# The first load of a row-normalising kernel cut into 16 and 112 partitions, and one row of the first tile moved between two forms of scaling

## The chip, the cores and the metric

The kernel runs on one core of one Trainium2 chip. The metric is the device time of one execution in microseconds (us). Times are read from repeated runs; the profile is one further execution, recorded by the hardware profiler, and its span is the time from its first to its last instruction.

## What is computed

The input has 32 x 512 rows of 1024 float32 numbers. Every row is divided by the sum of its absolute values:

```python
batch, seq, dim = 32, 512, 1024
...
sums = np.sum(np.abs(x), axis=-1, keepdims=True)
return (x / (sums + 1e-8)).astype(np.float32)
```

So 67.11 MB are read from memory, 67.11 MB are written back, and each number is used once for its sum and once for the division.

## The kernel before

The 16384 rows are taken as 128 per partition and cut into 11 tiles. Tiles 0 to 9 hold 12 rows for each of the 128 partitions (48 KB in each partition, 6.3 MB in all), and tile 10 holds the last 8. Tiles 0, 1 and 10 share one region of 32 rows per partition; within a tile the rows of one partition lie together in memory. Four tile buffers (`BUFS = 4`) are used in turn, so tile 4 can only be loaded when tile 0 has been stored.

The order is written out by hand. First the loads of tiles 0 to 3 are issued; then for each tile follow `compute(i)`, `store(i)` and, while tiles are left, `load(i + BUFS)`. All loads are issued from SyncE (SP, line 87), all stores from ScalarE's queue (ACT, line 97). A load or a store waits for the semaphores of what it needs, and what stands behind it in its queue waits too.

`max_dma_last_dim` sets the size of one piece of a transfer (a descriptor, seen in the trace as one packet): `WHOLE` is 49152 bytes, one partition's 12 rows; `HALF` is 24576. Tiles 0 and 1 are loaded with `WHOLE`, so the load of tile 0 is 128 packets of 48 KB, one for each partition. The store of tile 0 is cut in two: its first three rows (`FIRST = 3`) in packets of 4 KB, the other nine in packets of 36 KB.

`normalize` works on one tile. VectorE (DVE) sums the absolute values of all rows (L47), adds epsilon (L54) and takes the reciprocal (L56). The scaling of the rows is then divided in three, by `split`: some rows in one VectorE instruction that multiplies by a broadcast reciprocal (L58), some in single-row VectorE instructions (L65), and some in single-row ScalarE instructions (L68). An entry `split[i] = (kt, ks)` gives the number of single VectorE rows and of ScalarE rows; the rest go into the one large instruction. For tile 0 it is `(3, 4)`: five rows in one instruction, three single rows on VectorE, four on ScalarE. The first part of tile 0's store needs rows 0 to 2, which the large instruction writes.

Of the kernel before, what the change touches and what calls it, by code (L numbers as in the profile page):

```python
# [1 line left out]

# [4 lines left out]

FP32 = mybir.dt.float32
EPS = 1e-8


@with_exitstack
def kernel(
    ctx: ExitStack,
    tc: tile.TileContext,
    x: bass.AP,
    out: bass.AP,
):
    nc = tc.nc
    P = nc.NUM_PARTITIONS  # L20

    x_flat = x.flatten_outer_dims()
    out_flat = out.flatten_outer_dims()
    n, d = x_flat.shape

    R = 12
    BUFS = 4
    HEAD = 32
    per_partition = n // P
    assert n % P == 0 and (per_partition - HEAD) % R == 0  # L30
    rows = [R] * ((per_partition - HEAD) // R + 2) + [HEAD - 2 * R]

    def piece(flat, i):
        head = flat[: P * HEAD, :].rearrange("(p r) d -> p r d", p=P)
        if i < 2:
            return head[:, R * i : R * (i + 1), :]
        if i == len(rows) - 1:
            return head[:, 2 * R :, :]
        a = P * (HEAD + R * (i - 2))
        return flat[a : a + P * R, :].rearrange("(p r) d -> p r d", p=P)  # L40

    sbuf = ctx.enter_context(tc.tile_pool(name="sbuf", bufs=BUFS))
    stats = ctx.enter_context(tc.tile_pool(name="stats", bufs=len(rows)))

    def normalize(x_tile, k, kv, kt):
        s = stats.tile([P, R], FP32)
        nc.vector.tensor_reduce(  # L47
            out=s[:, :k],
            in_=x_tile[:, :k, :],
            axis=mybir.AxisListType.X,  # L50
            op=mybir.AluOpType.add,
            apply_absolute_value=True,
        )
        nc.vector.tensor_scalar_add(out=s[:, :k], in0=s[:, :k], scalar1=EPS)  # L54
        inv = stats.tile([P, R], FP32)
        nc.vector.reciprocal(out=inv[:, :k], in_=s[:, :k])  # L56
        if kv:
            nc.vector.tensor_mul(  # L58
                out=x_tile[:, :kv, :],
                in0=x_tile[:, :kv, :],  # L60
                in1=inv[:, :kv].unsqueeze(2).to_broadcast([P, kv, d]),
            )
        for r in range(kv, kv + kt):
            row = x_tile[:, r, :]
            nc.vector.tensor_scalar_mul(out=row, in0=row, scalar1=inv[:, r : r + 1])  # L65
        for r in range(kv + kt, k):
            row = x_tile[:, r, :]
            nc.scalar.activation(  # L68
                out=row,
                in_=row,  # L70
                func=mybir.ActivationFunctionType.Copy,
                scale=inv[:, r : r + 1],
            )

    last = len(rows) - 1
    split = {0: (3, 4), 1: (0, 3), 2: (0, 3), last - 1: (0, 2), last: (4, 4)}

    tiles = {}

    HALF, WHOLE = 24576, 49152
    FIRST = 3

    def load(i):
        x_tile = tiles[i] = sbuf.tile([P, R, d], FP32, name="x_tile")
        nc.sync.dma_start(out=x_tile[:, : rows[i], :], in_=piece(x_flat, i), max_dma_last_dim=WHOLE if i < 2 else HALF)  # L87

    def store(i):
        if i == 0:  # L90
            parts = [(0, FIRST, 4 * d), (FIRST, R, WHOLE)]
        elif i == last - 2:
            parts = [(0, R // 2, HALF), (R // 2, R, HALF)]
        else:
            parts = [(0, rows[i], WHOLE if i >= last - 1 else HALF)]
        for a, b, size in parts:
            nc.scalar.dma_start(
                out=piece(out_flat, i)[:, a:b, :],
                in_=tiles[i][:, a:b, :],
                max_dma_last_dim=size,  # L100
            )

    def compute(i):
        k = rows[i]
        kt, ks = split.get(i, (0, 0))
        normalize(tiles[i], k, k - kt - ks, kt)

    with tc.manual_schedule():
        for i in range(BUFS):
            load(i)  # L110
        for i in range(len(rows)):
            compute(i)
            store(i)
            if i + BUFS < len(rows):
                load(i + BUFS)


# [1 line left out]
_INS = ['x']  # L119
_OUTS = [((32, 512, 1024), 'float32')]  # L120


# [23 lines left out]
```

## Time and profile before

| what | value |
|---|---|
| time, median of 3 runs | 316.62 us (316.51 to 316.66) |
| span of the profiled execution | 315.2 us |
| difference of the two | 1.4 us outside the span |
| DMA, mean rate over the span | 426 GB/s, 134.22 MB |
| packets of the loads (queue q1) | 2736 |
| packets of the stores (queue q10) | 3024 |
| VectorE busy | 260.6 us, 83% |
| ScalarE busy | 18.5 us, 6% |

The profiled execution has no time of its own beside its span; what lies around the span is taken as the 1.4 us between it and the median. The page's second part cuts the span into 40 slices of 7.9 us; a digit is the busy share of an engine in tenths, and the last row is what the DMA engines moved. In tables of stretches, each row gives for one stretch its length, the busy time of each engine (with the number of instructions), the granted clock of TensorE (which has no work here), the DMA share (1.00 is all 16 DMA engines busy) and the rate. A packet is put down in the stretch in which it begins, so that a stretch shorter than a packet can show a share above 1 or a rate of 0.

### The profile page before, as it was taken

What the parts mean: (1) busy time and instruction counts of PE and PEld (TensorE: products, weight loads), DVE (VectorE), ACT (ScalarE), POOL (GpSimd) and SP (SyncE); (2) the same over time, 40 slices, a digit from 0 to 9 for tenths busy, and PEclk for the clock granted to TensorE, in tenths of its full rate; (3) what the DMA queues carried; (4) which work ended last, traced back from release to release, by engine and by line L of the source; (5) the groups of instructions that cost most, each with busy time, mean ns of one, the idle gap of its engine ahead of it and who ended that gap; (6) DMA issues with size and microseconds to landing.
All of it is one profiled execution on the core that took longest, in us unless ns stands there. A gap on an engine that the chain in (4) does not pass through costs nothing.

```text
span 315.2 us, 172 instructions
## 1 busy us (share of the span) xinstructions
DVE 260.6 (83%) x50; ACT 18.5 (6%) x17; POOL 0.2 (0%) x4
## 2 busy tenths in 40 slices
DVE  0079999999999999989996997999699969999000
ACT  0010503004000000000000000000000000203200
POOL 0000000000000000000000000000000000000000
DMA  8999999999999999999999999999999999999997
GB/s 318 480 399 412 437 407 464 411 436 413 415 446 437 415 446 437 415 449 434 415 449 437 412 449 437 412 449 437 415 446 437 415 437 434 432 428 496 399 408 324
DMA packets 5761, 134.22 MB, mean 426 GB/s; under 512 B 385, under 2 KB 385, under 8 KB 769
## 3 DMA queue, kind: packets, MB, share of 16 engines
q1 hardware_dynamic: 2736, 67.11, 49.8%
q10 hardware_dynamic: 3024, 67.11, 49.4%
q14 instruction: 1, 0.00, 0.0%
HBM read 67.11 MB, written 67.11 MB: 426 GB/s over the span
## 4 chain that ended last, share of the span: by engine, by line
DVE 40%; DMA 33%; another core or an unknown queue 18%; ACT 1%; issue 0%; SPq 0%
DVE s L47 23%; DMA x_tile<-in_x_dram 17%; DMA out_dram<-x_tile 16%; DVE x_tile L58 15%; ACT x_tile L68 1%; DVE x_tile L65 1%; DVE inv L56 0%; DVE s L54 0%; SPq L87 0%
## 5 line engine op out<-in xcount | busy, mean ns | idle before, releaser
L47 DVE TENSOR_REDUCE s<-x_tile 128x12 f32<-128x12288 f32 (+1 forms) x11 | 138.2, 12562 | 29.8 <-DMA x_tile<-in_x_dram 29.8
L58 DVE TENSOR_TENSOR x_tile<-x_tile,inv 128x12288 f32<-128x12288 f32 (+3 forms) x10 | 113.6, 11358 | 0.5
L68 ACT ACTIVATE x_tile<-x_tile,inv 128x1024 f32<-128x1024 f32 x16 | 17.2, 1138 | 256.9 <-DVE inv L56 256.9
L65 DVE TENSOR_SCALAR x_tile<-x_tile,inv 128x1024 f32<-128x1024 f32 x7 | 4.8, 749 | 0.0
L56 DVE RECIPROCAL inv<-s 128x12 f32<-128x12 f32 (+1 forms) x11 | 2.5, 226 | 0.4
L68 ACT ACT_TABLE_LOAD x1 | 1.3, 1283 | 17.8 <-DMA x_tile<-in_x_dram 17.8
L54 DVE TENSOR_SCALAR s<-s 128x12 f32<-128x12 f32 (+1 forms) x11 | 1.9, 174 | 0.4
L130 POOL MEMSET const-bfloat16-1.0<- 128x1 bf16 x1 | 0.1, 101 | 0.0
L130 POOL MEMSET const-uint8-127<- 128x1 uint8 x1 | 0.1, 101 | 0.0
L130 POOL MEMSET const-float32-0.0<- 128x1 f32 x1 | 0.1, 98 | 0.2 <-issue 0.2
L130 POOL MEMSET const-float32-1.0<- 128x1 f32 x1 | 0.1, 98 | 0.0
## 6 DMA issues: line engine op xcount, KB each, us to landing
x_tile<-in_x_dram SPq DMA_DIRECT2D x10, 6144.0 KB, 36.9
out_dram<-x_tile ACTq DMA_DIRECT2D x8, 6144.0 KB, 49.1
out_dram<-x_tile ACTq DMA_DIRECT2D x2, 3072.0 KB, 33.4
out_dram<-x_tile ACTq DMA_DIRECT2D x1, 4608.0 KB, 37.9
x_tile<-in_x_dram SPq DMA_DIRECT2D x1, 4096.0 KB, 32.2
out_dram<-x_tile ACTq DMA_DIRECT2D x1, 4096.0 KB, 20.9
out_dram<-x_tile ACTq DMA_DIRECT2D x1, 1536.0 KB, 29.3
```

Source lines behind the costliest of these rows:

```text
L47: nc.vector.tensor_reduce(out=s[:, :k], in_=x_tile[:, :k, :], axis=mybir.AxisListType.X, op=mybir.AluOpType.add, apply_absolute_value=True,)
L54: nc.vector.tensor_scalar_add(out=s[:, :k], in0=s[:, :k], scalar1=EPS)
L56: nc.vector.reciprocal(out=inv[:, :k], in_=s[:, :k])
L58: nc.vector.tensor_mul(out=x_tile[:, :kv, :], in0=x_tile[:, :kv, :], in1=inv[:, :kv].unsqueeze(2).to_broadcast([P, kv, d]),)
L65: nc.vector.tensor_scalar_mul(out=row, in0=row, scalar1=inv[:, r : r + 1])
L68: nc.scalar.activation(out=row, in_=row, func=mybir.ActivationFunctionType.Copy, scale=inv[:, r : r + 1],)
L130: nc = _bacc.Bacc("TRN2", target_bir_lowering=False, num_devices=1)
```

## The change

The load of tile 0 becomes two DMAs from the same queue: partitions 0 to 15 first, then partitions 16 to 127, still with 48 KB packets, one for each partition. The other loads and all stores are as they were. In the scaling of tile 0 the large VectorE instruction takes six rows instead of five, and two single rows instead of three are left on VectorE.

```diff
-    split = {0: (3, 4), 1: (0, 3), 2: (0, 3), last - 1: (0, 2), last: (4, 4)}
+    split = {0: (2, 4), 1: (0, 3), 2: (0, 3), last - 1: (0, 2), last: (4, 4)}
...
     FIRST = 3
+    AHEAD = 16
 
     def load(i):
         x_tile = tiles[i] = sbuf.tile([P, R, d], FP32, name="x_tile")
-        nc.sync.dma_start(out=x_tile[:, : rows[i], :], in_=piece(x_flat, i), max_dma_last_dim=WHOLE if i < 2 else HALF)
+        cuts = [(0, AHEAD), (AHEAD, P)] if i == 0 else [(0, P)]
+        for a, b in cuts:
+            nc.sync.dma_start(
+                out=x_tile[a:b, : rows[i], :],
+                in_=piece(x_flat, i)[a:b],
+                max_dma_last_dim=WHOLE if i < 2 else HALF,
+            )
```

## The prediction

> **What bounds the kernel now.** I read the page's busy times and slices first. VectorE works in 83% of the span, the DMA row stands at 9 in all but the first and the last slice.
>
> ```profile
> DVE 260.6 (83%) x50; ACT 18.5 (6%) x17; POOL 0.2 (0%) x4
> ...
> DMA  8999999999999999999999999999999999999997
> ```
>
> Then the busy time by stretches, to see whether the DMA engines ever wait for VectorE.
>
> ```profile
> 0.00:16.00 16.00, 0.00 (x0) 0.00 (x0) 0.20 (x4) 1.00 0.95 393
> ...
> 62.00:64.00 2.00, 2.00 (x1) 0.00 (x0) 0.00 (x0) 1.00 1.12 371
> 64.00:66.00 2.00, 2.00 (x1) 0.00 (x0) 0.00 (x0) 1.00 1.00 416
> 66.00:76.00 10.00, 9.90 (x4) 0.77 (x1) 0.00 (x0) 1.00 1.00 433
> ...
> 100.00:280.00 180.00, 167.18 (x26) 2.19 (x2) 0.00 (x0) 1.00 1.00 432
> ...
> 293.00:314.00 21.00, 0.00 (x0) 0.22 (x1) 0.00 (x0) 1.00 0.92 396
> ```
>
> The share is 1.00 for 180 us on end, at 432 to 433 GB/s. That is 27.1 GB/s for each of 16 engines, so a 48 KB packet takes 49152 B / 27.1 = 1.815 us, and 134.22 MB take 134.22 / 0.433 = 310.0 us. Of the 315.2 us span 5.2 are left: the start before the first packet, the landing of the last, and some slow packets. In the last 21 us VectorE does nothing and the DMA engines still drain stores: the last store is issued at 293.25 us by the timeline, 20 us before the end. So the time is that of the DMA engines. What VectorE does is covered by their queues; what delays the DMA engines in the first tile is never made up, because nothing later has slack.
>
> The chain of waits says the same for the start, and that the first tile has no compute beside it.
>
> ```profile
> 0.73 17.05 DMA x_tile<-in_x_dram
> 17.78 0.02 issue
> 17.80 12.96 DVE s L47
> ```
>
> Last I look at the first microseconds by themselves: the queues in 0 to 3 us, then short stretches.
>
> ```profile
> q1 hardware_dynamic: 16, 0.79, 84.9%
> ```
>
> ```profile
> 1.00:1.50 0.50, 0.00 (x0) 0.00 (x0) 0.00 (x0) 1.00 0.00 0
> 1.50:1.75 0.25, 0.00 (x0) 0.00 (x0) 0.00 (x0) 1.00 2.61 786
> 1.75:2.00 0.25, 0.00 (x0) 0.00 (x0) 0.00 (x0) 1.00 5.83 1769
> 2.00:2.50 0.50, 0.00 (x0) 0.00 (x0) 0.00 (x0) 1.00 0.88 295
> 2.50:3.00 0.50, 0.00 (x0) 0.00 (x0) 0.00 (x0) 1.00 0.00 0
> ```
>
> Packets are put down where they begin. Sixteen 48 KB packets, one per engine, begin between 1.5 and 2.5 us, about 1 us after the issue at 0.73; three of them (295 GB/s x 0.5 us = 0.147 MB) only after 2.0. The next packets begin after 4.0 us, so the first ones take over 2 us.
>
> **The change part by part.** *The scaling of tile 0.* The rows, by shape:
>
> ```profile
> L58 DVE TENSOR_TENSOR x_tile<-x_tile,inv 128x9216 f32<-128x9216 f32 x2 | 19.5, 9758 | 0.1
> ...
> L58 DVE TENSOR_TENSOR x_tile<-x_tile,inv 128x5120 f32<-128x5120 f32 x1 | 5.5, 5491 | 0.0
> L65 DVE TENSOR_SCALAR x_tile<-x_tile,inv 128x1024 f32<-128x1024 f32 x7 | 4.8, 749 | 0.0
> ```
>
> One row costs 9758/9 = 1.08 us to 5491/5 = 1.10 us in L58 and 0.75 in L65. Six rows take 6.5 to 6.6 us, 1.05 more; one single row less saves 0.75. Tile 0's scaling ends 0.3 us later and the first store, which waits for L58, is issued 1.05 us later (36.78 before). Behind it in ScalarE's queue stand the second part of that store, moved by 0.3, and the ScalarE rows of tile 1, which start at 52.1 us. At 36.8 us the loads of tiles 1 to 3 still fill the engines: four loads are 4 x 14.5 = 58 us of work, and with the store of tile 0 the engines are supplied to about 74 us, while tile 1 is stored at 62. I put this edit at 0. If the cover were gone it would cost 0.3 to 1.05 us. VectorE's 0.3 us goes into its own waits for loads: 29.8 us in six waits, 17.8 of them the first, so 12 later on.
>
> *The issue.* SP issues one DMA more. Its issues stand 0.42 us apart at the start (0.37 to 0.61 us each), so the loads of tiles 1 to 3 are issued some 0.4 us later, and the 112 partitions at about 1.1 us. Their packets would reach the engines by about 2.1 to 2.6 us, and the first ones are in work until 4.0: covered, 0. Each engine also ends one more DMA; packets of 4 bytes are all that adds.
>
> *The start of the first packets.* Sixteen descriptors instead of 128 may be handed out sooner. The first packets begin between 1.5 and 2.5 us, so the most that all could gain is some 0.6 us, and the least is nothing, or a loss of one issue, 0.4 us. I take a gain of 0.2.
>
> *The place of the first packets.* This is what I think decides. In every transfer of the trace 128 partitions take part, so the sixteen packets under way can lie all over SBUF, and the sum is 433 GB/s in every stage. The first piece puts sixteen packets on sixteen neighbouring partitions at the same moment. One partition takes a packet at the full 27.1 GB/s of an engine. Whether neighbours share a way in, no row shows. One end: they share nothing, the sixteen packets take 1.8 us, cost 0. The other: all sixteen share one way of 27.1 GB/s, 16 x 1.815 = 29.0 us, cost 27. The row that is nearest in size, the sixteen packets of the first 3 us, is spread over the partitions, which is the one thing that differs, so it can't choose. I take the middle in ratio, a factor of four: groups of four neighbours share, 4 x 1.815 = 7.3 us, **5.4 us more** on every engine, as each holds one of these packets at the head of its queue.
>
> [...]
>
> *The other 112.* With ways of 27.1 GB/s and 433 in all there are 16 ways, so 8 partitions to each. The first piece has used half of four of them; the other twelve still have 8 packets to take, 8 x 1.815 = 14.5 us where seven packets per engine alone are 12.7: 1.8 us more at the least, if the ways are never left idle. At the other end two engines always meet on one way, 12.7 us more. Engines that have drifted apart meet less, so I take 3.3, nearer to the lower end.
>
> Sum: 5.4 + 3.3 - 0.2 = 8.5 us. Against the profiled execution, 315.2 + 8.5 = 323.7 us of span, plus the 1.4 us outside it: 325.1, or 316.6 + 8.5 = **325.1 us**. Tile 0 would land at about 26 us instead of 17.8; VectorE, later by as much, has its 12 us of waits to give.
>
> **The rivals.** *Nothing shared (R1).* The packets of 48 KB go as fast to neighbours as elsewhere, or the rows keep the engines that they had in one transfer. For it speaks that a single partition takes the full rate, and that each engine has eight packets of tile 0 either way. Then only the start counts: 316.6 - 0.2 = 316.4, and it decides if the first sixteen packets end by 4.7 us as now. [...]
>
> *The start is worth more, and a stall goes (R2), on the faster side.* Between 62 and 66 us the rate is 371 and 416 instead of 433 GB/s: 62 and 17 GB/s too little for 2 us each, (124 + 34) / 433 = 0.36 us lost just when the loads run out and the first store ends. A first store that is 1.05 us later moves that meeting. With a start of 0.3 to 0.6 us earlier on the engine that is last now, 0.7 to 1.0 us in all: 315.8. Against it: the stall may as well grow by as much.
>
> *A small loss (R3).* The second load's packets come after the first have ended, or the 62 us stall doubles: 0.4 to 1 us, 317.4. It decides if engines idle between the two pieces, which the first packets' 2 us speak against.
>
> **How the numbers follow.** What a measurement of this kernel can tell is about 0.2%, 0.63 us. The place of the packets has most of the chance, 0.47, with its own range 320 to 329 (5.4 alone, less the start and some of the share, up to 5.4 + 7). R1 0.21, R2 0.27 and R3 0.05. R2 needs 0.63 us or more from a start and a stall that may each go either way; it stands above R1 because the rows hold up to 1 us to be won and R1's own 0.2 us would have to stay alone. So faster 0.28, same 0.20, slower 0.52. The range must hold both signs: 315.7 to 329.0 leaves out about 0.1 below (the better part of R2's upper gains) and 0.06 above.
>
> **What would show it.** If right, the first sixteen packets of the load queue end near 8 to 9 us instead of 4 to 4.7, so that the stretch from 4 to 8 us shows few new packets and a rate far below 400 GB/s; the chain's first DMA step is 24 to 29 us instead of 17.05; from 40 us on the rate is 432 again and the end is later by what was lost. L58 of tile 0 takes 6.5 us and nothing waits for it. If the first step of the chain stays at 17 us, sharing is refuted and R1 to R3 are left; then the first packets' starts and the rate in 62 to 66 us tell which. If tile 0 lands late and the end does not move, my view that nothing later has slack is wrong.

## The result, and the profile after

The changed kernel takes 331.86 us (median of 4 runs, 331.29 to 332.37) against 316.62: 15.24 us more, a ratio of 1.0482 (95% interval 1.047 to 1.0494). The profiled execution has a span of 330.1 us and a time of 331.71. Slower was forecast, by 8.5 us; the measured time lies above the range of 315.7 to 329.0 us that was given.

The page's busy times and slices, as before: busy share and number of instructions by engine, then 40 slices, now of 8.25 us each, with the DMA share in tenths and the rate.

```profile
DVE 261.0 (79%) x49; ACT 18.5 (6%) x17; POOL 0.2 (0%) x4
...
DMA  9997999999999999999999999999999999999896
GB/s 137 244 268 208 465 390 429 438 441 425 438 432 432 429 432 429 438 426 432 432 429 435 438 429 435 432 438 432 429 435 432 429 428 442 434 435 474 387 449 262
```

The rates of the kernel before, in its slices of 7.9 us:

```profile
GB/s 318 480 399 412 437 407 464 411 436 413 415 446 437 415 446 437 415 449 434 415 449 437 412 449 437 412 449 437 415 446 437 415 437 434 432 428 496 399 408 324
```

VectorE's work is what it was, 261.0 us. The DMA row alone would show next to nothing: the engines count as busy at 9, 9, 9 and 7 in the first four slices. The row under it shows the loss: 137 to 268 GB/s in these slices where the kernel before had 318 to 480, then the old 430 or so. With the share near 1 at half the rate, time in which a packet is held up counts as busy, so the busy share must be read with the rate.

The busy time by stretches of the changed kernel (length, busy time of DVE, ACT and POOL, clock, DMA share, GB/s):

```profile
0.00:16.00 16.00, 0.00 (x0) 0.00 (x0) 0.20 (x4) 1.00 1.02 194
16.00:32.00 16.00, 0.00 (x0) 0.00 (x0) 0.00 (x0) 1.00 0.94 243
32.00:36.00 4.00, 2.39 (x1) 1.28 (x1) 0.00 (x0) 1.00 0.92 393
...
62.00:64.00 2.00, 2.00 (x1) 0.00 (x0) 0.00 (x0) 1.00 1.01 434
64.00:66.00 2.00, 2.00 (x1) 0.00 (x0) 0.00 (x0) 1.00 1.04 444
...
100.00:280.00 180.00, 167.59 (x26) 0.00 (x0) 0.00 (x0) 1.00 1.00 432
```

The kernel before in the second of these stretches (the first, at 393 GB/s, stands in the prediction):

```profile
16.00:32.00 16.00, 14.10 (x4) 2.02 (x2) 0.00 (x0) 1.00 0.97 418
```

In the first 32 us 7.0 MB move where before 393 and 418 GB/s made 13.0 MB of them; the missing 6.0 MB are 13.8 us of work at 433 GB/s. From 40 us on the rate is back: 427 GB/s in 40 to 62 us (422 before) and 432 from 100 to 280 us, as before. The start of the chain of waits of the changed kernel (start, length, what):

```profile
1.17 32.34 DMA x_tile<-in_x_dram
...
33.61 12.96 DVE s L47
...
47.06 6.56 DVE x_tile L58
```

Tile 0 is summed from 33.6 us on instead of 17.8, 15.8 us later. The last packet of tile 0 ends 15.0 us later (at 32.5 us instead of 17.4), and the span is 14.9 us longer. The queue of the loads in the first 3 us of the changed kernel has the same sixteen packets and bytes as before:

```profile
q1 hardware_dynamic: 16, 0.79, 206.1%
```

The last number is the time of these packets as a share of 16 engines' 3 us: 2.061 x 3 = 6.2 us for each, where 84.9% meant 2.5. In the trace the last of them ends at 8.7 us instead of 4.75, and the 112 packets of the second piece follow with 3.29 us on average instead of 1.82. So for each engine the first packet costs 6.18 - 2.55 = 3.6 us more, and the seven others 23.0 - 12.7 = 10.3 us.

### The profile page after: what moved, and what is told of

Its sections match the earlier page's. It is cut to its first block, busy times and chain, and to the rows that moved or that the text cites. A ratio compares the mean times of both kernels' runs of the same rounds, so it can differ in the third digit from the quotient of the medians.

```text
span 330.1 us, 174 instructions
## 1 busy us (share of the span) xinstructions
DVE 261.0 (79%) x49; ACT 18.5 (6%) x17; POOL 0.2 (0%) x4
## 4 chain that ended last, share of the span: by engine, by line
DVE 38%; DMA 36%; another core or an unknown queue 17%; ACT 1%; SPq 0%; issue 0%; DVEq 0%
DVE s L47 22%; DMA x_tile<-in_x_dram 21%; DVE x_tile L58 15%; DMA out_dram<-x_tile 14%; ACT x_tile L68 1%; DVE inv L56 0%; DVE x_tile L65 0%; SPq L90 0%; DVE s L54 0%; DVEq L47 0%
## 5 line engine op out<-in xcount | busy, mean ns | idle before, releaser
L47 DVE TENSOR_REDUCE s<-x_tile 128x12 f32<-128x12288 f32 (+1 forms) x11 | 138.2, 12562 | 45.2 <-DMA x_tile<-in_x_dram 45.2
L58 DVE TENSOR_TENSOR x_tile<-x_tile,inv 128x12288 f32<-128x12288 f32 (+3 forms) x10 | 114.6, 11465 | 0.5
L68 ACT ACT_TABLE_LOAD x1 | 1.3, 1283 | 33.6 <-DMA x_tile<-in_x_dram 33.6
```

The source lines that it names most:

```text
L47: nc.vector.tensor_reduce(out=s[:, :k], in_=x_tile[:, :k, :], axis=mybir.AxisListType.X, op=mybir.AluOpType.add, apply_absolute_value=True,)
L58: nc.vector.tensor_mul(out=x_tile[:, :kv, :], in0=x_tile[:, :kv, :], in1=inv[:, :kv].unsqueeze(2).to_broadcast([P, kv, d]),)
L68: nc.scalar.activation(out=row, in_=row, func=mybir.ActivationFunctionType.Copy, scale=inv[:, r : r + 1],)
```

## The experiments

**Each edit alone.** The split alone, with one load of tile 0:

```diff
-    split = {0: (3, 4), 1: (0, 3), ...
+    split = {0: (2, 4), 1: (0, 3), ...
```

> Only the scaling of tile 0 is changed, to one instruction of six rows and two single rows; its load is one DMA as before. Theory A (the place: packets under way at the same moment to neighbouring partitions share a way into SBUF, and the scaling is hidden): 316.6 us, within 0.4 either way; tile 0 lands at 17.8 us. Theory B (the cut matters only together with the later first store): 318 us or more already here. The stall at 62 to 66 us (371 and 416 GB/s before) may move by up to 0.4 us in either direction.

Measured: 316.81 us (316.60 to 316.93), ratio 1.0005 (0.9997 to 1.0014). The split is no part of the 15 us. The stall of 62 to 66 us moved:

```profile
62.00:64.00 2.00, 2.00 (x2) 0.00 (x0) 0.00 (x0) 1.00 1.31 455
64.00:66.00 2.00, 2.00 (x1) 0.00 (x0) 0.00 (x0) 1.00 0.86 367
```

These are the two stretches with the split alone: 455 and 367 GB/s, in sum a loss of (66 x 2 - 22 x 2) / 433 = 0.2 us where before there were 0.36.

The cut alone, with the scaling as before (`split = {0: (3, 4), ...`, load as in the changed kernel):

> Only the load of tile 0 is cut, into partitions 0 to 15 and 16 to 127; the scaling is as before (five rows, three single ones). Theory A: 331.9 us within 0.6, the whole loss, tile 0 landing at 33 to 34 us. Theory B (both edits needed): clearly under 330.

Measured: 331.93 us, ratio 1.0483 (1.0469 to 1.0498), the whole loss.

**Cut by rows instead of partitions.**

```diff
-    AHEAD = 16
+    AHEAD = 2
...
-        cuts = [(0, AHEAD), (AHEAD, P)] if i == 0 else [(0, P)]
+        cuts = [(0, AHEAD), (AHEAD, R)] if i == 0 else [(0, rows[i])]
...
-                out=x_tile[a:b, : rows[i], :],
-                in_=piece(x_flat, i)[a:b],
+                out=x_tile[:, a:b, :],
+                in_=piece(x_flat, i)[:, a:b, :],
```

> The load of tile 0 is two DMAs again, but cut by rows: the first two rows of all 128 partitions (packets of 8 KB), then the other ten (packets of 40 KB). Scaling as before. Theory A: 316.6 us within 0.4, since both DMAs take part in all 128 partitions; tile 0 lands at 17 to 18.5 us. Theory C (a second DMA on the first tile costs by itself, by its issue or its completion, wherever it writes): 325 us or more, tile 0 landing after 26 us.

Measured: 317.30 us (317.04 to 317.63), ratio 1.0021 (1.0013 to 1.0030); tile 0 is there at 17.8 us.

```profile
1.16 16.64 DMA x_tile<-in_x_dram
```

(The chain of waits of that kernel.) A second DMA as such does not delay tile 0. The 0.7 us is more than the 0.4 that I allowed. By the medians of the runs 0.3 of it lies in the span (315.3 against 315.0 us) and the rest outside it; the cause was not followed up.

**The memory side.** The 48 KB pieces of neighbouring partitions are put 48 KB apart in memory, with the cut at 16 partitions kept:

```diff
+        if i == 0:
+            return flat[: P * R, :].rearrange("(p r) d -> p r d", p=P)
+        if i == 1:
+            return flat[P * R : 2 * P * R, :].rearrange("(p r) d -> p r d", p=P)
+        if i == len(rows) - 1:
+            return flat[2 * P * R : P * HEAD, :].rearrange("(p r) d -> p r d", p=P)
```

> The changed kernel, with tiles 0, 1 and 10 taken from three regions of the input of their own, so that the 48 KB pieces of neighbouring partitions lie 48 KB apart in memory instead of 128 KB; the places in SBUF are the same. Theory A: 331.9 us within 1, the first sixteen packets take over 5 us each and the next 2.5 to 5. Theory D (the memory side: pieces 128 KB apart for neighbouring partitions are read from few channels): most of the 15 us goes, under 322 us.

Measured: 332.20 us, ratio 1.0491 (1.0475 to 1.0507). The sixteen first packets take 6.1 us, the others 3.36 on average. Theory D falls.

**Loads one at a time.** Thirteen loads stand ahead of the kernel before; VectorE reads a little of each before the next may start, so its wait (`DVE looked`) is the time from issue to landing:

```python
nc.sync.dma_start(out=probe[where], in_=what, max_dma_last_dim=WHOLE)
nc.vector.tensor_reduce(out=s[:, :1], in_=probe[:, :1, :], ...)
```

> Thirteen loads are put ahead of the kernel before, one at a time (each waits until VectorE has read from the one before it); all in 48 KB packets, so the kernel's own time is some 200 us longer and only the time from issue to landing of each is read. A load of 128 partitions has a fixed part of about 2.5 us (17.05 less 8 x 1.815). In this order: 128 partitions; 16 neighbours from memory pieces 128 KB, 48 KB and 512 KB apart; 16 partitions in steps of 2, of 4 and of 8 (memory 128 KB apart); the 112 partitions 16 to 127 with 128 and 48 KB; 32, 64, 96 and 128 partitions from 0. Theory A1 (a way in belongs to four neighbouring partitions and all engines go at the pace of the fullest way): 17; 9.8 three times; steps of 2: 6.1, of 4 and of 8: 4.3; 112: 16 to 26; 32: 9.8; 64: 9.8; 96: 13 to 24; 17. [...] Theory D (memory side): the three of 16 neighbours differ by over 2 us, and the steps cost as much as the neighbours.

VectorE's timeline, cut to ten of the loads; the number before "<-DMA" is what counts. In this order: 128 partitions; 16 neighbours with 128, 48 and 512 KB between the pieces; steps of 2, of 4, of 8; the 112; 64; 96.

```profile
17.78 1.22 DVE L132 TENSOR_REDUCE looked<-x_tile 128x1 f32<-128x1024 f32 x1 [17.78 <-DMA x_tile<-in_x_dram]
28.24 1.22 DVE L132 TENSOR_REDUCE looked<-x_tile 128x1 f32<-128x1024 f32 x1 [9.24 <-DMA x_tile<-in_x_dram]
39.15 1.22 DVE L132 TENSOR_REDUCE looked<-x_tile 128x1 f32<-128x1024 f32 x1 [9.69 <-DMA x_tile<-in_x_dram]
49.58 1.22 DVE L132 TENSOR_REDUCE looked<-x_tile 128x1 f32<-128x1024 f32 x1 [9.21 <-DMA x_tile<-in_x_dram]
57.18 1.22 DVE L132 TENSOR_REDUCE looked<-x_tile 128x1 f32<-128x1024 f32 x1 [6.39 <-DMA x_tile<-in_x_dram]
64.61 1.22 DVE L132 TENSOR_REDUCE looked<-x_tile 128x1 f32<-128x1024 f32 x1 [6.21 <-DMA x_tile<-in_x_dram]
72.16 1.22 DVE L132 TENSOR_REDUCE looked<-x_tile 128x1 f32<-128x1024 f32 x1 [6.32 <-DMA x_tile<-in_x_dram]
99.20 1.22 DVE L132 TENSOR_REDUCE looked<-x_tile 128x1 f32<-128x1024 f32 x1 [25.83 <-DMA x_tile<-in_x_dram]
...
157.15 1.22 DVE L132 TENSOR_REDUCE looked<-x_tile 128x1 f32<-128x1024 f32 x1 [17.72 <-DMA x_tile<-in_x_dram]
182.70 1.22 DVE L132 TENSOR_REDUCE looked<-x_tile 128x1 f32<-128x1024 f32 x1 [24.33 <-DMA x_tile<-in_x_dram]
```

Not shown are the 112 with 48 KB between the pieces (26.99 us), 32 partitions (9.58) and the last load of all 128 (16.93; the first began with the program). Sixteen neighbours take 9.2 to 9.7 us at each of the three distances in memory; the same bytes spread over SBUF in steps of 2, 4 and 8 take 6.2 to 6.4. A1 does not hold: by it the steps of 4 and of 8 would be at 4.3 us, where 6.21 and 6.32 were measured, and 64 partitions at 9.8 instead of 17.72. The steps of 4 and of 8 take what the steps of 2 take (6.39), in which two neighbours of each four are under way, as if each of their packets, too, met one other. What fits the times of the neighbours, the steps and the 64 is that every four neighbours share their way with the four that lie 32 further on, in the lower 64 partitions and in the upper 64 alike; the next expectation calls it A2. It is inferred from the times, as the trace names no way. In all, 64 partitions take about as long as 128, and 96 or 112 take 24 to 27, longer than all 128. The 26.99 and the 24.33 for 96 lie somewhat above the 16 to 26 and 13 to 24 that A1 allowed.

**A cut at 64.** `AHEAD = 64` in the changed kernel:

> The changed kernel with the cut at partition 64: two loads of 64 partitions, four packets per engine each. Theory A1 (way of four neighbours alone): the sixteen engines are on sixteen different fours, 316.6 to 318 us. Theory A2 (partitions 32 apart share too): two packets on each way all the time, eight steps of 3.63 instead of 1.815 us, 14.5 us more, 331 us. Theory E (only the sixteen neighbours of the first piece are bad, and the 112 behind them suffer from its disorder): under 321 us.

Measured: 331.92 us, ratio 1.0485 (1.0470 to 1.0501), near A2's 331 and not A1's 316.6 to 318. Two loads without the sixteen cost the same 15.3 us. In the trace all packets after the first of each engine take 3.60 to 3.85 us; the stretches:

```profile
0.00:16.00 16.00, 0.00 (x0) 0.00 (x0) 0.20 (x4) 1.00 0.94 197
16.00:32.00 16.00, 0.00 (x0) 0.00 (x0) 0.00 (x0) 1.00 0.96 200
```

**The cut in the middle of the run.** `if i == 6` instead of `if i == 0`, scaling as before:

> The load of tile 0 is one DMA again and the scaling as before; instead the load of tile 6, in the middle of the run beside stores, is cut into partitions 0 to 15 and 16 to 127 (two packets of 24 KB per partition). Theory A with engines that stand still behind a full way: the same loss as in tile 0, 14 to 16 us, 331 us. Theory F (an engine that waits for a way into SBUF works on a store meanwhile): the loss is half of it or less, under 324 us.

Measured: 323.64 us, ratio 1.0230 (1.0213 to 1.0247): 7.0 us, less than half. The stretches around that load, issued at 131 us (433, 434 and 432 GB/s in the same stretches before):

```profile
138.00:148.00 10.00, 9.01 (x1) 0.00 (x0) 0.00 (x0) 1.00 0.99 258
148.00:168.00 20.00, 17.30 (x4) 0.00 (x0) 0.00 (x0) 1.00 1.01 413
168.00:200.00 32.00, 23.72 (x4) 0.00 (x0) 0.00 (x0) 1.00 1.00 430
```

The rate falls to 258 GB/s at first and is then close to full. The time is the one that F gave, but F's reason is not what the trace shows. From 138 to 145 us, with the sixteen partitions under way, the loads move 0.81 MB instead of 1.50, and the stores beside them do not gain but lose, 0.91 MB instead of 1.45; a store packet takes 1.23 us on average instead of 0.91. The 112 behind them run almost at the old pace, 0.98 us per packet against 0.91, where in tile 0 they took 1.8 times the old. With stores on the same engines fewer load packets are under way at once, so fewer may meet on one way; that is an explanation which no run here tests.

**The first piece without the second.** A load of 16 partitions into the buffer of tile 3 ahead of the whole loads of the kernel before:

```diff
+            nc.sync.dma_start(out=tiles[3][:16, :, :], in_=piece(x_flat, 0)[:16], max_dma_last_dim=WHOLE)
```

> The kernel before, with its whole loads, and ahead of them one more load of 16 partitions (0 to 15, 48 KB packets), into the buffer of tile 3, which tile 3's own load overwrites later; 0.79 MB more are moved. It prices the first piece alone, with no 112 behind it. From the lone loads (16 partitions 6.2 us for its packets, whole loads 1.8 us per packet): the first packets take 6.2 instead of 2.5 us and each engine moves one packet more, 3.7 + 1.8 = 5.5 us, 322.1 us. Theory G (the second piece is the larger part, 11 of 15 us): 322.1 within 1. Theory H (the disorder left by the sixteen slows whatever comes behind): whole loads behind it are slow too, 326 us or more.

Measured: 323.01 us, ratio 1.0207 (1.0190 to 1.0224), 6.4 us: 0.9 more than summed, within the bound of G. Of it 1.8 is the extra packet of each engine, so 4.6 us are the price of the sixteen. Behind them the whole load of tile 0 is at 1.82 us per packet from each engine's second packet on (the median of the first ones is 2.83). H falls, and some 10.7 us of the 15.3 are left for the 112.

**Smaller packets.** In the changed kernel, tile 0 in packets of 24 KB (`WHOLE if i == 1 else HALF`):

> The changed kernel with tile 0's two pieces in packets of 24 KB instead of 48 KB, two for each partition. Theory G1 (two engines are on one way nearly all the time because the ways hold all engines to one pace, whatever the size of a packet): 331.9 within 1. Theory G2 (engines that could change places more often would drift apart and meet less, as my 3.3 us assumed): under 328 us.

Measured: 332.12 us, ratio 1.0492 (1.0476 to 1.0507). G2 falls. The time agrees with G1, but does not show G1's reason.

**Ways filled unequally.** A second series of loads one at a time, built as the first:

> Eight loads ahead of the kernel before, one at a time, 48 KB packets, memory pieces 128 KB apart; read are the sixteen packets of each. In this order: 128 partitions; 0 to 15; sixteen in steps of 7 from 16 (by the 16 ways found so far, twelve alone on a way and four in two pairs; it is what the second piece of the changed kernel would have under way at first if each engine takes seven partitions in a row); in steps of 7 from 18 (fourteen alone, one pair); in steps of 3 from 0 (nine of them three to a way, three alone); in steps of 5 from 0; in steps of 8 from 0; 128 partitions. Theory J (each engine at the pace of its own way): in the steps of 7 the packets that are alone take 2.5 us as in a whole load and only the four, or two, that share take 3.5; in steps of 3 packets of 2.5 to 5.5 us side by side. Theory K (all sixteen engines held to the pace of the fullest way): steps of 7 all 3.3 to 3.7, steps of 3 all 4.5 to 5.5, and the second piece of 112 must then run at a pair's pace from end to end.

| partitions | on a way, counted by A2 | 16 packets, shortest to longest |
|---|---|---|
| 0 to 15 | four on each of 4 | 5.4 to 6.9 us |
| 16, 23, ... 121 | two pairs, 12 alone | 2.7 to 3.4 us |
| 18, 25, ... 123 | one pair, 14 alone | 1.9 to 2.6, and two at 3.1 and 3.3 |
| 0, 3, ... 45 | nine in threes, 4 in pairs, 3 alone | 4.2 to 6.1 us |
| 0, 5, ... 75 | 10 in pairs, 6 alone | 3.2 to 4.0 us |
| 0, 8, ... 120 | all in pairs | 2.9 to 4.1 us |
| 128 partitions, first 16 | (whole load) | 1.9 to 2.8 us |

(The counts of pairs and threes follow from A2; for the steps of 3 my expectation left out the four in pairs.) With one pair only two packets are slow, as J says; with two pairs or more nearly all sixteen are slower than in a whole load, as K says, and in the steps of 3 the three that are alone take at least 4.2 us. Neither theory holds throughout. The second line is within 2.7 to 3.4, so twelve packets that are alone on their way gain little from it. Each line is one load.

The 112 have left the same mark. Alone, in the first series, the medians of their seven rounds of sixteen packets are 3.27, 3.45, 2.34, 2.89, 3.29, 3.48 and 3.21 us: the third and the fourth are the shorter ones (rounds are counted in order of start). If each engine takes seven partitions in a row, engine e is at partition 16 + 7e + j in round j (j from 0), and A2 gives two pairs in every round but the third and the fourth, which have one; the fourth, at 2.89, is still longer than the table has for one pair. The trace names no partition of a packet, so this order is inferred from the pattern, not seen. All 128 can't be dealt out like this: by A2 eight partitions in a row would put two engines on each of eight ways in every round, by estimate 8 x 3.63 = 29 us, and the packets of a whole load take 15.7. How it is dealt out, no run here shows.

The size of the loss also asks for engines that hold each other up. With that order, 1.815 us per packet and two packets on a way sharing it equally, engines that wait for nothing but their own way would have the 112 in some 16 us and both pieces in some 24; if every round took as long as a pair, it would be 7 x 3.63 = 25.4 us and 7.3 + 25.4 = 32.7. These are estimates. Measured, from the first packet's begin to the last one's end, are 24.2 us for the 112 alone and 30.7 for both pieces in the changed kernel.

## Why the prediction was right and wrong

- *What bounds the kernel*: right. The last packet of tile 0 ends 15.0 us later, the time is 15.2 us longer, and nothing in between makes it up. VectorE's 12 us of later waits were not needed: 45.2 - 33.6 = 11.6 of them are still there, as the later loads are late too.
- *The scaling of tile 0 at 0*: right, 316.81 us for it alone. Of its terms, six rows in L58 were put at 6.5 to 6.6 us:

```profile
L58 DVE TENSOR_TENSOR x_tile<-x_tile,inv 128x6144 f32<-128x6144 f32 x1 | 6.6, 6558 | 0.0
```

- *The issue at 0*: right; SP issues the second piece 0.44 us after the first, and the row cut, with the same two issues, has tile 0 at its old time.
- *A start sooner by 0.2 us*: wrong. Sixteen descriptors were not handed out sooner than 128: the first packets begin between 1.76 and 2.51 us, before between 1.74 and 2.40. In short stretches of the changed kernel none begins before 1.75 us, and some after 2.5:

```profile
1.50:1.75 0.25, 0.00 (x0) 0.00 (x0) 0.00 (x0) 1.00 0.00 0
1.75:2.00 0.25, 0.00 (x0) 0.00 (x0) 0.00 (x0) 1.00 17.28 2163
2.00:2.50 0.50, 0.00 (x0) 0.00 (x0) 0.00 (x0) 1.00 2.96 393
2.50:3.00 0.50, 0.00 (x0) 0.00 (x0) 0.00 (x0) 1.00 0.76 98
```

- *The place of the first packets, 5.4 us*: right in kind and nearly in size. Sixteen neighbours take longer than sixteen partitions spread over SBUF (9.2 to 9.7 us against 6.2 to 6.4, issue to landing), and the sixteen packets end between 7.4 and 8.7 us, near the 8 to 9 that were to show it. The sixteen packets take 6.9 us from the first begin to the last end, where 4 x 1.815 = 7.3 was the price; as the whole packet was compared with 1.8 and not with the 2.5 that a first packet takes anyway, the term came out at 3.6 (trace of the changed kernel) to 4.6 us (the sixteen with whole loads behind). The price was for neighbours alone; the steps of 4 (6.21 us, not A1's 4.3) and the cut at 64 (331.92 us, not A1's 316.6 to 318) show that packets to partitions further apart slow each other too.
- *The other 112, 3.3 us*: this is the term that failed, with 10.3 us in the trace and 10.7 as the rest of the runs. The step was "Engines that have drifted apart meet less, so I take 3.3, nearer to the lower end", in a span of 1.8 to 12.7. That step let each engine wait for its own way alone, so that those without a partner would run on freely. The runs show instead that the engines hold each other up: with two pairs on the ways, counted by A2, the other twelve are slowed as well (2.7 to 3.4 us, against 1.9 to 2.8 in a whole load), and smaller packets change nothing (332.12 us). The forecast's 14.5 + 5.4 + 3.3 = 23.2 us for both pieces is about what engines that wait for their own way alone would need (some 24 by the estimate above); the trace has 30.7, and the chain's DMA step is 32.34 us where 24 to 29 were to show. The mean packet of 3.29 us is 1.8 times that of a whole load, near the upper end of the term. What makes one engine wait for another stays open.
- With these two terms the sum is 3.6 + 10.3 = 13.9 us for the mean engine; the end of tile 0's last packet, which counts, moves from 17.4 to 32.5 us, 15.0 later, as the engines do not end together. The range, 329.0 at the top, had "5.4 + 7" for the upper case and so cut off the upper end of the second term, which stood in the text at 12.7.
- *The rivals*: R1, R2 and R3 needed a load of tile 0 at its old time and fall by the chain. With the split alone R2's stall shrinks from 0.36 to 0.2 us, and the time does not fall (316.81 us). In the changed kernel the loads run out at another time, so its 434 and 444 GB/s between 62 and 66 us do not tell whether the stall is gone.

## What to carry to other kernels

A load that names only part of the partitions can take longer than the whole: 96 or 112 partitions in 48 KB packets took 24 to 27 us where all 128 took 17, and two halves one behind the other landed at 33.9 us instead of 17.8. Where a first tile is to come in pieces, cut it along the rows of each partition (0.7 us here, and not 15), and look in the profile at the rate and not at the busy share, since packets that are held up count as busy (a share of 1.02 at 194 GB/s here). When a cost is bounded from two sides and the lower end needs the engines to arrange themselves well, let the range reach the upper end; here the cost lay near it.

## What the runs showed of the hardware that was not expected

In one load each, with the ways counted by A2, one pair of packets on a shared way slowed only itself (3.1 and 3.3 us beside fourteen of 1.9 to 2.6), while two pairs lengthened nearly all sixteen (2.7 to 3.4, against 1.9 to 2.8 in a whole load). What holds the others was not found. The same cut cost 15.3 us in tile 0 and 7.0 in tile 6, where stores run beside it: there the sixteen partitions slowed the stores too (1.23 us per packet instead of 0.91), while the 112 ran almost at the old pace.
